# 896 of 2048 columns of the first expert layer as dense products, and one-hot products that pick each slot's value

## The chip, the cores and the metric

The kernel runs on one NeuronCore of one Trainium2 chip. Five engines work side by side, each through its own queue in order: TensorE (PE, matrix products, with its weight loads as PEld), VectorE (DVE), ScalarE (ACT), GpSimd (POOL) and SyncE (SP, which only starts transfers). Transfers run on 16 DMA engines; they come from a queue that SP or ScalarE fills, or from GpSimd's, which alone makes gathers by a list of rows. What is compared is the device time of one execution in microseconds (us), the median of several.

## What is computed

One encoder layer over 256 tokens and 16 meta tokens of width 2048: a gated linear attention and a differential attention, merged and projected by `w_out`, then an expert layer, then a last norm. Only the expert layer, `peer`, is touched. It has 16,384 experts, each a row of `u_tab` and a row of `v_tab`, and 8 heads; a head takes for each token the 16 best experts of a 128 by 128 grid of key pairs:

```python
qb = (xb @ w_q).reshape(TB, PEER_HEADS, 2, PEER_DKEY)
s = jnp.einsum('thpc,hpnc->thpn', qb, sub_keys)
sv, si = lax.top_k(s, K)                       # K = 16
cand = (sv[:, :, 0, :, None] + sv[:, :, 1, None, :]).reshape(TB, PEER_HEADS, K * K)
cidx = (si[:, :, 0, :, None] * PEER_NKEYS + si[:, :, 1, None, :]).reshape(TB, PEER_HEADS, K * K)
cv, ci = lax.top_k(cand, K)
eidx = jnp.take_along_axis(cidx, ci, axis=-1)
g = jax.nn.softmax(cv, axis=-1)
a = jax.nn.gelu(jnp.einsum('thkd,td->thk', u_tab[eidx], xb))
return jnp.einsum('thk,thkd->td', g * a, v_tab[eidx])
```

So each token has 128 slots (8 heads of 16), each slot an expert i * 128 + j. The step that the change rewrites is the inner product of `u_tab[eidx]` with the token's normalized row, 2048 columns for 256 x 128 slots.

## The kernel before

The 256 tokens are two tiles of 128, `tt` = 0 and 1; a tile's tokens lie on the 128 partitions. After the attention branches and the projection by `w_out`, whose result is `hs`, the expert layer runs in these steps.

- **Queries** (`queries`, L778): for each head, products with `w_q` on TensorE (three passes over weights split into high and low parts, L185 and L186), the scores against the sub-keys (L790), and for the first tile `route` at once.
- **Routing** (`route`, L714): top 16 twice over and once more over the 256 sums, nearly all on VectorE, with two casts (L721, L732) and a product (L736) on GpSimd and an exponential (L743) on ScalarE. Its last instruction, L739, writes the 16 row numbers of the head. The second tile's routing needs only the scores `sS1`, which stay in SBUF, and stands between the gathers of the first tile.
- **Gathers** (`gather_dots`, L745): for each slot GpSimd issues one gather (L751) of 128 rows of 2048 floats, 1 MB, and VectorE multiplies them by the normalized tokens `xb` and sums them into one column of `dots` (L754). There are 2 x 128 of them. Six buffers hold rows: three of tag `g` and three of tag `raw`, by turns.
- **Weights** (`weights_of`, L757): gelu of `dots`, times the softmax; then i, j and the weight of each slot are transposed, so that slots lie on the partitions.
- **W0 and W1**: for each token a 128 by 128 matrix with the weight of expert (i, j) at its place, the product of two one-hot matrices over the slots. `build_w0` (L809) makes all its one-hots on ScalarE, and stands between the gathers of the second tile; `build_w1` (L823) shares them between VectorE, GpSimd and ScalarE and comes after the gathers. W0 and W1 take 64 KB of each partition each.
- **The second expert layer** (from L876): for most columns a dense product of W0 and W1 with all of `v_tab`, four accumulators of 368 columns at a time (L924 to L926), the weights split again (L897, L898); for 576 columns gathers of rows (L884) with VectorE's multiply and add (L887). Then the last norm.

The order of instructions of one engine is fixed when the program is built, by a scheduler that follows data and the order in the code. An engine that waits holds up all that stands behind it in its queue. 

Of the kernel before, what the change touches and what calls it, by code (L numbers as in the profile page):

```python
# [20 lines left out]
P = 128  # L21
# [19 lines left out]
def block_kernel(ctx: ExitStack, tc: tile.TileContext, A: dict, out: bass.AP):  # L41
# [12 lines left out]
    s3 = pool("s3")  # L54
    wpc = ExitStack()
    wp = pool("wp", side="right", c=wpc)
# [4 lines left out]
    bt = pool("bt")  # L61
# [28 lines left out]
    mhalf = cc[:, 257:258]  # L90
    vr = c1.tile([58, P], F32, name="vr")
# [545 lines left out]
    wk.close()  # L637


    rp = pool("rp", side="right", c=rgt)  # L640
    ringc = ExitStack()
    ring = pool("ring", bufs=3, side="right", c=ringc)
# [28 lines left out]
    for tt in range(2):  # L671
        nc.gpsimd.dma_start(xb[:, tt, :], A["g_ffn"].to_broadcast([P, D]))
    sk = ring.tile([P, 16, P], F32, tag="g", name="sk")
# [18 lines left out]
    sS1 = rp.tile([P, 8, 2, P], F32, name="sS1")  # L692
# [11 lines left out]
    ngather = [0]  # L704
# [9 lines left out]
    def route(tt, h, s_):  # L714
# [18 lines left out]
        ohx = rp.tile([P, 2, 16, 16], F32, tag="ohx", name="ohx", bufs=1)  # L733
# [12 lines left out]
    def gather_dots(tt, h, ei):  # L746
        for k in range(16):
            i = ngather[0]
            ngather[0] += 1
# [7 lines left out]
    def weights_of(tt):  # L757
# [5 lines left out]
        nc.scalar.activation(dots[tt], dots[tt], AF.Gelu)  # L763
        nc.vector.tensor_mul(gw[tt], gw[tt], dots[tt])  # L764
        ps = pa([P, 3, P])
        nc.tensor.transpose(ps[:, 0, :], ij[tt][:, 0, :], ident)
        nc.tensor.transpose(ps[:, 1, :], ij[tt][:, 1, :], ident)
        nc.tensor.transpose(ps[:, 2, :], gw[tt], ident)  # L768
        r = bt.tile([P, 3, P], F32, tag=f"b{2 + tt}", name=f"slotT{tt}")
        nc.scalar.activation(r, ps, AF.Copy)  # L770
        return r
# [3 lines left out]
    wait = [(None, ring), (None, ring), (None, [4, 5, 6, 7]), (None, [8, 9, 10, 11]), (None, [12, 13, 14, 15])] + [None] * 3  # L775
    eis = {}

    def queries(h):  # L778
# [6 lines left out]
        s0 = rp.tile([P, 2, P], F32, tag="sS0", name="sS0", bufs=2)  # L785
        with tc.high_priority():
            for tt in range(2):
# [4 lines left out]
                nc.scalar.activation(s0 if tt == 0 else sS1[:, h], ps, AF.Copy, scale=rst[tt])  # L792
# [16 lines left out]
    def build_w0(wt, sT, t4):  # L809
        ps = pa([P, 4, P])  # L810
        oh = wp.tile([P, 2, 4, P], F32, tag="hi", name="oh0", bufs=3)
        for q in range(4):
            t = t4 * 4 + q
            for a in range(2):
                nc.scalar.activation(oh[:, a, q], iota, AF.Abs, bias=sT[:, a, t:t + 1], scale=-1.0)
        nc.scalar.activation(oh, oh, AF.Relu, bias=onec, scale=-1.0)
        for q in range(4):
            t = t4 * 4 + q
            nc.scalar.activation(oh[:, 0, q], oh[:, 0, q], AF.Copy, scale=sT[:, 2, t:t + 1])  # L819
            nc.tensor.matmul(ps[:, q, :], lhsT=oh[:, 1, q], rhs=oh[:, 0, q], start=True, stop=True)  # L820
        nc.scalar.activation(wt[:, :, t4 * 4:t4 * 4 + 4], ps.rearrange("p t i -> p i t"), AF.Copy)

    def build_w1(vp, wt, sT, nj, t4):  # L823
        ps = pa([P, 4, P])
        for q2 in range(2):
# [14 lines left out]
            for q in range(2):  # L840
                oi = vp.tile([P, P], F32, tag="oi1", name="oi1", bufs=4)
# [5 lines left out]
    for h in range(8):  # L847
        gather_dots(0, h, eis[0, h])
        eis[1, h] = route(1, h, sS1[:, h])
    w0p = pool("w0p")  # L850
    W0 = w0p.tile([P, P, P], F32, name="W0")
# [142 lines left out]
def host_vectors(inputs):  # L994
# [5 lines left out]
    for nm in ("w_branch_gla", "w_branch_diff", "w_out", "peer_w_q"):  # L1000
        r["c_" + nm] = host_blocks(np.asarray(inputs[nm])[0], 256)
    return r


def host_constants():
# [4 lines left out]
    cf[:, 257] = -0.5  # L1010
    msk = np.zeros((P, 3, T), np.int32)
# [41 lines left out]
```

## Time and profile before

| | us |
|---|---|
| median of 3 runs | 2612.32 (2608.33 to 2615.7) |
| the profiled execution | 2616.36 |
| its span, first to last instruction | 2614.6 |
| TensorE busy | 1889.1 |
| VectorE busy | 2132.0 |
| GpSimd busy | 1266.1 |
| ScalarE busy | 1106.8 |

The page divides the span into 40 slices of 65 us. A row of the views of time has the start in us from the span's start, the duration, the engine, the line and the operation, the tile written and those read, the shape, and how many equal instructions were joined; in brackets stands the idle time of that engine just before, and what ended it. A joined row's duration reaches from the first start to the last end. A matrix product of f32 operands counts as two records. The view of stretches gives the busy time of each engine, the clock that was granted to TensorE as a share of full speed (1.00 is 2.4 GHz, 0.50 is 1.2 GHz), the busy share of the DMA engines, and what they moved.

### The profile page before, as it was taken

What the parts mean: (1) busy time and instruction counts of PE and PEld (TensorE: products, weight loads), DVE (VectorE), ACT (ScalarE), POOL (GpSimd) and SP (SyncE); (2) the same over time, 40 slices, a digit from 0 to 9 for tenths busy, and PEclk for the clock granted to TensorE, in tenths of its full rate; (3) what the DMA queues carried; (4) which work ended last, traced back from release to release, by engine and by line L of the source; (5) the groups of instructions that cost most, each with busy time, mean ns of one, the idle gap of its engine ahead of it and who ended that gap; (6) DMA issues with size and microseconds to landing.
All of it is one profiled execution on the core that took longest, in us unless ns stands there. A gap on an engine that the chain in (4) does not pass through costs nothing. (4 is left out here: it accounts for less than half of the span.)

```text
span 2614.6 us, 37107 instructions
## 1 busy us (share of the span) xinstructions
PE 1889.1 (72%) x13809; PEld 1835.5 (70%) x13809; DVE 2132.0 (82%) x2921; ACT 1106.8 (42%) x2076; POOL 1266.1 (48%) x989
## 2 busy tenths in 40 slices
PE   8999999999999999997500000143006999999997
PEld 7999999999999999997500000132005888999897
DVE  4778877557777775559999999996978899999998
ACT  4565554345655544443200000698006344444444
POOL 1333310000110001028876888885856777777775
PEclk9999999999999999998855555566558999999999
DMA  4445445554444465656699899997993788889886
GB/s 160 146 147 178 146 148 199 187 181 164 165 157 166 167 237 180 227 198 213 227 350 347 322 375 422 421 421 298 418 357 117 263 304 301 315 302 306 302 300 240
DMA packets 110913, 658.38 MB, mean 252 GB/s; under 512 B 14514, under 2 KB 17132, under 8 KB 53116
## 3 DMA queue, kind: packets, MB, share of 16 engines
q0 software_dynamic: 59216, 348.40, 35.2%
q1 hardware_dynamic: 51312, 307.45, 33.8%
q8 instruction: 108, 1.77, 0.3%
q14 instruction: 73, 0.60, 0.1%
q10 hardware_dynamic: 204, 0.17, 0.0%
HBM read 652.78 MB, written 2.10 MB: 250 GB/s over the span
## 5 line engine op out<-in xcount | busy, mean ns | idle before, releaser
L186 DVE TENSOR_TENSOR lo<-raw,hi 128x1024 fp32r<-128x1024 f32 x354 | 453.2, 1281 | 242.7 <-ACT hi L185 240.9
L202 PE MATMUL pm<-hT,lo 128*128 128x256 f32 (+1 forms) x2048 | 577.9, 285 | 7.9 <-DVE lo L186 7.9
L200 PE MATMUL pm<-hT,hi 128*128 128x256 f32 (+1 forms) x2048 | 581.8, 285 | 0.0
L201 PE MATMUL pm<-hT,hi 128*128 128x256 f32 (+1 forms) x2048 | 581.6, 285 | 0.0
L185 ACT ACTIVATE hi<-raw 128x1024 fp32r<-128x1024 f32 x374 | 395.9, 1059 | 363.3 <-PE pm L201 292.5
L202 PEld LDWEIGHTS pm<-hT,lo 128*128 128x128 f32 x2048 | 384.9, 189 | 10.7 <-DVE lo L186 9.0
L200 PEld LDWEIGHTS pm<-hT,hi 128*128 128x128 f32 x2048 | 386.0, 188 | 0.3
L201 PEld LDWEIGHTS pm<-hT,hi 128*128 128x128 f32 x2048 | 386.1, 189 | 0.2
L884 POOL DMA_INDIRECT gv<-in_peer_v_dram,ent x256 | 309.6, 1209 | 140.9 <-DVE hs L887 87.1
L754 DVE SCALAR_TENSOR_TENSOR g<-g,xb 128x2048 f32<-128x2048 f32 x128 | 326.4, 2553 | 15.6 <-DMA g<-in_peer_u_dram,ent 15.3
L768 PE MATMUL pa<-cc,gwt 128*128 128x128 f32 x2 | 0.9, 474 | 462.3 <-DVE gwt L764 462.3
L926 PE MATMUL acc<-vhi,wb 128*128 128x368 f32 x1024 | 334.2, 331 | 0.8 <-DVE wb L898 0.8
L768 PEld LDWEIGHTS pa<-cc,gwt 128*128 128x128 f32 x2 | 0.4, 181 | 462.9 <-DVE gwt L764 462.9
L754 DVE SCALAR_TENSOR_TENSOR gr<-gr,xb 128x2048 f32<-128x2048 f32 x128 | 295.3, 2309 | 28.8 <-DMA gr<-in_peer_u_dram,ent 28.8
L887 DVE SCALAR_TENSOR_TENSOR hs<-gv,gwt,hs 128x576 f32<-128x576 f32 x256 | 280.3, 1095 | 39.3 <-DMA gv<-in_peer_v_dram,ent 35.0
L751 POOL DMA_INDIRECT gr<-in_peer_u_dram,ent x128 | 259.0, 2023 | 78.6 <-DVE gr L754 33.5
L751 POOL DMA_INDIRECT g<-in_peer_u_dram,ent x128 | 250.3, 1956 | 82.4 <-DVE g L754 31.2
L926 PEld LDWEIGHTS acc<-vhi,wb 128*128 128x128 f32 x1024 | 192.4, 189 | 1.0 <-DVE wb L898 1.0
L925 PE MATMUL acc<-vlo,wb 128*128 128x368 f32 x512 | 172.9, 342 | 18.0 <-DVE vlo L917 9.2
L925 PE MATMUL acc<-vlo,wwv 128*128 128x368 f32 x512 | 172.3, 341 | 15.0 <-DVE vlo L917 10.4
L539 POOL DMA_DIRECT2D sw<-dqT x8 | 4.5, 563 | 287.1 <-ACT dqT L552 175.0
L820 PE MATMUL pa<-oh 128*128 128x128 f32 x256 | 58.1, 408 | 104.2 <-ACT oh L819 102.8
(876 smaller groups left out, 4610.6 us busy)
## 6 DMA issues: line engine op xcount, KB each, us to landing
raw<-in_c_w_in_dram SPq DMA_DIRECT2D x128, 1024.0 KB
raw<-in_c_w_branch_gla_dram SPq DMA_DIRECT2D x16, 1024.0 KB
raw<-in_c_w_branch_diff_dram SPq DMA_DIRECT2D x16, 1024.0 KB
raw<-in_c_w_out_dram SPq DMA_DIRECT2D x16, 1024.0 KB
raw<-in_c_peer_w_q_dram SPq DMA_DIRECT2D x11, 1024.0 KB
gv<-in_peer_v_dram,ent POOLq DMA_INDIRECT x256
raws<-in_c_peer_w_q_dram SPq DMA_DIRECT2D x12, 256.0 KB
xt<-in_x_dram SPq DMA_DIRECT2D x2, 1024.0 KB
```

Source lines behind the costliest of these rows:

```text
L185: nc.scalar.activation(hi[:, ks], raw, AF.Copy)
L186: (lo_eng or nc.vector).tensor_sub(lo[:, ks], raw, hi[:, ks].bitcast(F32))
L200: nc.tensor.matmul(ps[b], lhsT=wh, rhs=ah, start=(k == 0), stop=False)
L201: nc.tensor.matmul(ps[b], lhsT=wh, rhs=al, start=False, stop=False)
L202: nc.tensor.matmul(ps[b], lhsT=wl, rhs=ah, start=False, stop=(k == KT - 1))
L751: nc.gpsimd.indirect_dma_start(out=g, out_offset=None, in_=u_tab, in_offset=bass.IndirectOffsetOnAxis(ap=ei[:, k:k + 1], axis=0))
L754: nc.vector.scalar_tensor_tensor(g, g, 1.0, xb[:, tt, :], op0=ALU.mult, op1=ALU.mult, accum_out=dots[tt][:, s:s + 1])
L820: nc.tensor.matmul(ps[:, q, :], lhsT=oh[:, 1, q], rhs=oh[:, 0, q], start=True, stop=True)
L884: nc.gpsimd.indirect_dma_start(out=g, out_offset=None, in_=v_tab, in_offset=bass.IndirectOffsetOnAxis(ap=eis[tt, s // 16][:, s % 16:s % 16 ...
L887: nc.vector.scalar_tensor_tensor(hs[:, tt, DC:], g, gw[tt][:, s:s + 1], hs[:, tt, DC:], op0=ALU.mult, op1=ALU.add)
L925: nc.tensor.matmul(o, lhsT=wh[:, tt, :], rhs=lo[:, ns], start=False, stop=False)
L926: nc.tensor.matmul(o, lhsT=wl[:, tt, :], rhs=hi[:, ns], start=False, stop=last(tt))
```

## The change

The first 896 columns of the first expert layer are no longer gathered. They are computed for all 16,384 experts and all 256 tokens as a dense product, and the value that belongs to a slot is then taken out of it.

- `gather_dots` fetches columns 896 to 2047 of a row (`element_offset`), 1152 floats, 589,824 bytes a gather, into five buffers of one tag; `xb` keeps only these columns.
- A transposed normalized copy of the first 896 columns, `hn`, is made by small products after the third head's queries. The table's first 896 columns come transposed by the host, `c_uT`, as 128 tiles of 128 x 7 x 128 floats (458,752 bytes), through SP's queue into three buffers. For each tile seven products of 128 x 128 by 256 tokens (L911) run in f32; two tiles make a group with one PSUM tile, and ScalarE copies it into `Y`, which is W0 for the first 128 tokens and W1 for the second.
- `pick` takes four tokens at a time. Four products (L782) spread the slots' j over the partitions, ScalarE turns them into one-hots in two passes (L784, L785), four products (L789) select the row j of `Y` for each slot, and four instructions on VectorE (L790) select column i and sum into `dT`. It is called 32 times for each tile.
- `weights_of` adds `dT` to the gathered part; `dots` and the softmax weights are transposed for it, and the result is transposed back.
- W0 can be built only when its `Y` has been read. Both builds are now the same function, `build_w`, with the one-hots shared between VectorE, GpSimd and ScalarE as in `build_w1`.
- To make room, the scores of the second tile and `hs` go to DRAM and come back (ScalarE's queue), pools are opened and closed elsewhere, and the first heads' `w_q` no longer borrows the gathers' buffers.

```diff
-    xb = s4.tile([P, 2, D], F32, tag="s4", name="xb")
+    xb = rp.tile([P, 2, D - DU], F32, name="xb")
+    hn = rp.tile([P, KU, T], F32, name="hn")
...
-    sS1 = rp.tile([P, 8, 2, P], F32, name="sS1")
+    sS1d = [drp.tile([P, 2, P], F32, name=f"sS1d{h}") for h in range(8)]
+    hsd = drp.tile([P, 2, D], F32, name="hsd")
...
-            g = ring.tile([P, D], F32, tag="g", name="g") if i % 2 else wp.tile([P, D], F32, tag="raw", name="gr", bufs=3)
+            g = ring.tile([P, D - DU], F32, tag="g", name="g", bufs=NG)
             nc.gpsimd.indirect_dma_start(out=g, out_offset=None, in_=u_tab,
-                                         in_offset=bass.IndirectOffsetOnAxis(ap=ei[:, k:k + 1], axis=0))
+                                         in_offset=bass.IndirectOffsetOnAxis(ap=ei[:, k:k + 1], axis=0),
+                                         element_offset=DU)
...
+    def pick(tt, sT, t4):
+        pj = pa([P, 4, P])
+        for q in range(4):
+            t = t4 * 4 + q
+            nc.tensor.matmul(pj[:, q, :], lhsT=identr[:, t:t + 1].to_broadcast([P, P]), rhs=jr[:, tt], start=True, stop=True)
+        oj = rp.tile([P, 4, P], F32, tag="ohx", name="ojT", bufs=2)
+        nc.scalar.activation(oj, pj, AF.Abs, bias=mrow, scale=1.0)
+        nc.scalar.activation(oj, oj, AF.Relu, bias=onec, scale=-1.0)
+        pz = pm([P, 4, P])
+        for q in range(4):
+            t = t4 * 4 + q
+            nc.tensor.matmul(pz[:, q, :], lhsT=oj[:, q, :], rhs=Y[tt][:, :, t], start=True, stop=True)
+            nc.vector.scalar_tensor_tensor(pz[:, q, :], iota, sT[:, 0, t:t + 1], pz[:, q, :], op0=ALU.is_equal, op1=ALU.mult,
+                                           accum_out=dT[:, tt, t:t + 1])
...
+    def weights_of(tt, sT):
...
+        nc.vector.tensor_add(dT[:, tt], dT[:, tt], ps[:, 0, :])
+        nc.scalar.activation(dT[:, tt], dT[:, tt], AF.Gelu)
+        nc.vector.tensor_mul(sT[:, 2], dT[:, tt], ps[:, 1, :])
...
+            nc.scalar.dma_start(sS1d[h], s_)
...
     for h in range(8):
         gather_dots(0, h, eis[0, h])
-        eis[1, h] = route(1, h, sS1[:, h])
...
-    sT0 = weights_of(0)
+        s_ = rp.tile([P, 2, P], F32, tag="sS", name="sS", bufs=3)
+        nc.scalar.dma_start(s_, sS1d[h])
+        eis[1, h] = route(1, h, s_)
+
+    for g in range(P // 2):
+        ps = pm([P, 2, T])
+        for b in range(2):
+            ur = ep.tile([P, KU, P], F32, tag="ur", name="ur", bufs=3)
+            nc.sync.dma_start(ur, A["c_uT"][2 * g + b])
+            for k in range(KU):
+                nc.tensor.matmul(ps[:, b, :], lhsT=ur[:, k, :], rhs=hn[:, k, :], start=(k == 0), stop=(k == KU - 1))
+        for tt in range(2):
+            nc.scalar.activation(Y[tt][:, 2 * g:2 * g + 2, :], ps[:, :, tt * P:(tt + 1) * P], AF.Copy)
     for h in range(8):
         gather_dots(1, h, eis[1, h])
-        for t4 in range(4 * h, 4 * h + 4):
-            build_w0(W0, sT0, t4)
-    sT1 = weights_of(1)
...
+    sTs = [slots_of(tt) for tt in range(2)]
+    for tt in range(2):
+        sT = sTs[tt]
+        for t4 in range(32):
+            pick(tt, sT, t4)
+        weights_of(tt, sT)
...
+        if tt == 0:
+            for t4 in range(32):
+                build_w(ep.tile([P, 4, P], F32, tag="ur", name="oi4", bufs=3), W0, sT, nj, t4)
...
-            build_w1(vp, W1, sT1, nj1, t4)
+            build_w(vp.tile([P, 4, P], F32, tag="gv", name="oi4", bufs=NGV), W1, sT1, nj1, t4)
```

How the instructions then stand on an engine is seen from lists of the two programs. On VectorE, before, at the last gathers of the second tile: L754 is the multiply-and-sum, L764 the product with the softmax, L842 and L837 the one-hots of W1's build.

```order
L754 SCALAR_TENSOR_TENSOR gr,gwt<-gr,xb 128x2048 x2
L754 SCALAR_TENSOR_TENSOR g,gwt<-g,xb 128x2048 x2
L754 SCALAR_TENSOR_TENSOR gr,gwt<-gr,xb 128x2048 x16
L764 TENSOR_TENSOR gwt<-gwt 128x128
L864 TENSOR_SCALAR ent<-slotT_16846 128x128
L842 TENSOR_SCALAR oi_16868<-cc,slotT_16846 128x128
L842 TENSOR_SCALAR oi_16871<-cc,slotT_16846 128x128
L842 TENSOR_SCALAR oi_16878<-cc,slotT_16846 128x128
L842 TENSOR_SCALAR oi_16881<-cc,slotT_16846 128x128
L837 TENSOR_TENSOR oj_16886<-cc,slotT_16846 128x256
```

After it, VectorE's queue at the same place: L764 is now the multiply-and-sum, L750 the last instruction of the routing, L790 the selection in `pick`, L802 and L804 are in `weights_of`, L894 is the one-hot in the build of W0.

```order
L764 SCALAR_TENSOR_TENSOR g,gwt<-g,xb 128x1152
L750 SCALAR_TENSOR_TENSOR ent<-ijt 128x16
L923 TENSOR_SCALAR ent<-slotT_17632 128x128
L764 SCALAR_TENSOR_TENSOR g,gwt<-g,xb 128x1152 x170
L790 SCALAR_TENSOR_TENSOR pm,dT<-cc,slotT_17626,pm 128x128 x128
L802 TENSOR_TENSOR dT<-dT,pa 128x128
L804 TENSOR_TENSOR slotT_17626<-dT,pa 128x128
L894 TENSOR_SCALAR oi_18195<-cc,slotT_17626 128x128 x4
L894 TENSOR_SCALAR oi_18213<-cc,slotT_17626 128x128 x4
```

What moved: behind the last gather stood the build of W1; now 128 selections and the build of W0 stand there, and after these a second 128 selections and the build of W1. Ahead of L750 (before: L739) stand 86 multiply-and-sums, and before it was 93.

On TensorE in the changed kernel, from the last product of the dense layer (L911, into PSUM tiles `pm`) on; L789 selects row j of `Y` (here W0) with the one-hot tile `ojT`, and L782 spreads the j of four tokens:

```order
L911 MATMUL pm_17221<-hn_12574,ur_17222 128x256 x7
L911 MATMUL pm_17221<-hn_12574,ur_17231 128x256 x7
L789 MATMUL pm_17646<-W0_15184,ojT_17643 128x128
L789 MATMUL pm_17663<-W0_15184,ojT_17660 128x128
L789 MATMUL pm_17646<-W0_15184,ojT_17643 128x128
L789 MATMUL pm_17663<-W0_15184,ojT_17660 128x128
L789 MATMUL pm_17646<-W0_15184,ojT_17643 128x128
L789 MATMUL pm_17663<-W0_15184,ojT_17660 128x128
L789 MATMUL pm_17646<-W0_15184,ojT_17643 128x128
L789 MATMUL pm_17663<-W0_15184,ojT_17660 128x128
L782 MATMUL pa_17740<-jr_15169,identr_15167 128x128 x4
L782 MATMUL pa_17757<-jr_15169,identr_15167 128x128 x4
```

The products of two calls of `pick` stand by turns, two one-hot tiles a pair, and the spreading for a later pair behind them. On ScalarE the same pairs stand so, behind the last copies of the dense layer (L913; L784 and L785 are the two passes over a one-hot tile):

```order
L913 ACTIVATE W0_15184<-pm_17221 128x256
L913 ACTIVATE W1_15185<-pm_17221 128x256
L784 ACTIVATE ojT_17677<-pa_17672,cc_94 128x512
L784 ACTIVATE ojT_17694<-pa_17689,cc_94 128x512
L785 ACTIVATE ojT_17677<-ojT_17677,cc_94 128x512
L785 ACTIVATE ojT_17694<-ojT_17694,cc_94 128x512
L784 ACTIVATE ojT_17711<-pa_17706,cc_94 128x512
L784 ACTIVATE ojT_17728<-pa_17723,cc_94 128x512
L785 ACTIVATE ojT_17711<-ojT_17711,cc_94 128x512
L785 ACTIVATE ojT_17728<-ojT_17728,cc_94 128x512
```

Nothing stood at either place before; at this point of the program TensorE and ScalarE had the last of W0's one-hots and products.

## Rows read from the trace of the kernel before

**Rows 1.** The page: TensorE's busy tenths in 40 slices of the span.
```profile
PE   8999999999999999997500000143006999999997
```

**Rows 2.** Busy time by stretch; columns as the first line says.
```profile
core 0: us, PE busy (x) PEld busy (x) DVE busy (x) ACT busy (x) POOL busy (x), PEclk, DMA share, GB/s
1200.00:1538.00 338.00, 65.59 (x448) 61.93 (x446) 333.12 (x617) 29.27 (x66) 272.65 (x157) 0.61 0.82 302
1538.00:1801.00 263.00, 48.97 (x217) 43.76 (x217) 243.25 (x215) 142.45 (x400) 228.70 (x107) 0.56 1.01 420
1801.00:1823.00 22.00, 9.80 (x42) 9.02 (x42) 0.63 (x2) 19.92 (x52) 1.39 (x2) 0.63 0.42 175
...
1975.00:2024.00 49.00, 41.88 (x262) 37.05 (x263) 47.00 (x150) 42.63 (x98) 32.42 (x50) 0.94 0.25 81
```

**Rows 3.** Timeline, all engines: the wait for L898 (start, duration, instruction, idle before).
```profile
1822.37 0.42 DVE L898 TENSOR_TENSOR wb<-W,wb 128x256 fp32r<-128x256 f32 x1 [21.72 <-ACT wb L897]
...
1825.28 2.75 POOL L751 DMA_INDIRECT g<-in_peer_u_dram,ent  x1 [22.58 <-DVE g L754]
```

**Rows 4.** Timeline: the end of the last gather's sum, then the first one-hot behind it.
```profile
1975.06 0.09 DVE L754 DVE_READ_ACCUMULATOR gr<-gr,xb 128x1 f32 x1
...
1977.04 1.26 DVE L842 TENSOR_SCALAR oi<-cc,slotT 128x128 f32<-128x128 f32 x4
```

**Rows 5.** Timeline of VectorE: gathered rows multiplied and summed.
```profile
1540.22 0.08 DVE L754 DVE_READ_ACCUMULATOR gr<-gr,xb 128x1 f32 x1
1540.22 2.29 DVE L754 SCALAR_TENSOR_TENSOR g<-g,xb 128x2048 f32<-128x2048 f32 x1
...
1542.43 2.29 DVE L754 SCALAR_TENSOR_TENSOR g<-g,xb 128x2048 f32<-128x2048 f32 x1
```

**Rows 6.** Groups by line, GpSimd, 1200 to 1538: count | busy, mean ns | idle before.
```profile
L751 POOL DMA_INDIRECT g<-in_peer_u_dram,ent x53 | 93.4, 1763 | 33.3 <-DVE g L754 7.0 <-issue 4.9 <-DVE sv L711 4.7
```

**Rows 7.** Timeline of TensorE: 128x128 f32 products at full clock.
```profile
1168.57 0.61 PE L790 MATMUL pa<-skT,pqt 128*128 128x128 f32 x4
1169.01 0.71 PE L685 MATMUL pa<-cc,sk 128*128 128x128 f32 x5
```

**Rows 8.** DMA view of 1560 to 1600, then of 2100 to 2300 (packets, MB, share).
```profile
DMA packets 2312, 16.84 MB, mean 421 GB/s; under 512 B 256, under 2 KB 256, under 8 KB 256
...
DMA packets 13696, 61.27 MB, mean 306 GB/s; under 512 B 2142, under 2 KB 2142, under 8 KB 13552
...
q1 hardware_dynamic: 6681, 35.24, 51.2%
q0 software_dynamic: 6999, 25.82, 37.1%
```

**Rows 9.** Timeline of GpSimd's gather issues; last L884's durations (min/median/max).
```profile
1541.41 1.91 POOL L751 DMA_INDIRECT gr<-in_peer_u_dram,ent  x1 [0.30 <-issue]
...
1770.95 0.94 POOL L751 DMA_INDIRECT gr<-in_peer_u_dram,ent  x1 [0.30 <-issue]
...
L884 POOL DMA_INDIRECT gv<-in_peer_v_dram,ent x256: 945/1146/2227, 2021.2 to 2587.3; - x128
```

**Rows 10.** Timeline of ScalarE: evaluations of 512 columns from PSUM, of 128 and 1024 from SBUF.
```profile
1811.43 0.65 ACT L821 ACTIVATE W<-pa 128x512 f32<-128x512 f32 x1
1811.91 2.22 ACT L815 ACTIVATE oh<-cc,slotT 128x128 f32<-128x128 f32 x7
1813.95 0.66 ACT L821 ACTIVATE W<-pa 128x512 f32<-128x512 f32 x1
...
1814.72 2.25 ACT L816 ACTIVATE oh<-oh,cc 128x1024 f32<-128x1024 f32 x2
1816.80 0.76 ACT L819 ACTIVATE oh<-oh,slotT 128x128 f32<-128x128 f32 x2
```

**Rows 11.** Timeline of VectorE: two instructions of 256 elements from PSUM.
```profile
1082.73 0.88 DVE L668 SCALAR_TENSOR_TENSOR hg<-pa,vec,hg 128x256 fp32r<-128x256 f32 x2 [1.26 <-ACT hg L667]
```

**Rows 12.** Timeline of TensorE in the build of W1.
```profile
1996.00 1.81 PE L844 MATMUL pa<-oi,oj 128*128 128x128 f32 x12 [0.19 <-DVE oi L842]
```

More of the change, by code (lines that the diff above doesn't have):

```diff
@@ L53, in block_kernel @@
     cst = pool("cst")
-    s3 = pool("s3")
+    bt = pool("bt")
+    s3c = ExitStack()
+    s3 = pool("s3", c=s3c)
     wpc = ExitStack()
-    wp = pool("wp", side="right", c=wpc)
+    wp = wr = pool("wp", side="right", c=wpc)
+    drp = pool("drp", space=bass.MemoryType.DRAM)
     psA = ctx
@@ L637, in block_kernel @@
     wk.close()
+    rgt.close()
+    wpc.close()
+    KU = 7
+    DU = KU * P
+    rgt = ExitStack()
     rp = pool("rp", side="right", c=rgt)
-    ringc = ExitStack()
-    ring = pool("ring", bufs=3, side="right", c=ringc)
+    ring = pool("ring", side="right", c=rgt)
+    wpc = ExitStack()
+    wp = pool("wp2", side="right", c=wpc)
+    wr = pool("wr2", side="right", c=wpc)
     hs = s3.tile([P, 2, D], F32, tag="s3", name="hs")
     ssq = cst.tile([P, 2, 8], F32, name="ssq")
-    xb = s4.tile([P, 2, D], F32, tag="s4", name="xb")
+    xb = rp.tile([P, 2, D - DU], F32, name="xb")
+    hn = rp.tile([P, KU, T], F32, name="hn")
     hg = [None] * KT
@@ L703, in block_kernel @@
     u_tab = A["peer_u"][0]
-    ngather = [0]
+    NG = 5
     def top16(vo, io, src, n):
@@ L755, in gather_dots, with slots_of @@
                                            accum_out=dots[tt][:, s:s + 1])
-    def weights_of(tt):
+    def slots_of(tt):
+        r = bt.tile([P, 3, P], F32, tag=f"b{2 + tt}", name=f"slotT{tt}")
+        ps = pa([P, 2, P])
+        for a in range(2):
+            nc.tensor.transpose(ps[:, a, :], ij[tt][:, a, :], ident)
+        nc.scalar.activation(r[:, 0:2], ps, AF.Copy)
+        nc.scalar.activation(jr[:, tt], ij[tt][:, 1, :], AF.Copy)
+        return r
+    def pick(tt, sT, t4):
[13 more added lines that the diff above has]
+    def weights_of(tt, sT):
         rc = rp.tile([P, 8], F32, tag="rcs", name="rcs", bufs=2)
@@ L799, in block_kernel, with build_w @@
     for tt in range(2):
-        nc.vector.scalar_tensor_tensor(xb[:, tt, :], hs[:, tt, :], rst[tt], xb[:, tt, :], op0=ALU.mult, op1=ALU.mult)
+        nc.vector.scalar_tensor_tensor(xb[:, tt, :], hs[:, tt, DU:], rst[tt], xb[:, tt, :], op0=ALU.mult, op1=ALU.mult)
+    nc.scalar.dma_start(hsd, hs)
     for h in range(1, 8):
         queries(h)
+        if h == 2:
+            dg = []
+            for tt in range(2):
+                d_ = wp.tile([P, P], F32, tag="hi", name="dgr", bufs=3)
+                nc.vector.tensor_scalar(d_, ident, rst[tt], None, op0=ALU.mult)
+                dg.append(d_)
+            for k in range(KU):
+                ps = pa([P, T])
+                for tt in range(2):
+                    nc.tensor.matmul(ps[:, tt * P:(tt + 1) * P], lhsT=hs[:, tt, k * P:(k + 1) * P], rhs=dg[tt], start=True,
+                                     stop=True)
+                nc.scalar.activation(hn[:, k, :], ps, AF.Copy, scale=vec[:, gf + k:gf + k + 1])
+    identr = rp.tile([P, P], F32R, name="identr")
+    nc.scalar.activation(identr, ident, AF.Copy)
+    jr = rp.tile([P, 2, P], F32R, name="jr")
+    dT = rp.tile([P, 2, P], F32, name="dT")
+    nj0 = rp.tile([P, P], F32, name="nj0")
+    wpc.close()
     ph0.close()
     ph1.close()
-    W1E = "pav"
[L809 to L823, printed above, removed]
+    s3c.close()
+    wp01 = pool("w01")
+    epc = ExitStack()
+    ep = pool("ep", side="right", c=epc)
+    W0 = wp01.tile([P, P, P], F32, name="W0")
+    W1 = wp01.tile([P, P, P], F32, name="W1")
+    Y = [W0, W1]
+    W1E = "pav"
+    def build_w(oi4, wt, sT, nj, t4):
         ps = pa([P, 4, P])
```

60 lines of the change are left out of this document (30 added, 30 removed).

## The prediction

> **What bounds the kernel now.** I read TensorE's slices first [rows 1], then the busy time of each engine by stretch [rows 2], then single instructions inside the stretches. The first 1200 us (18 slices) and the last 590 us keep TensorE nine tenths busy, and the change hardly touches them. Between 1200 and 1975 us lies what it does touch: TensorE is almost idle, and VectorE, GpSimd and the DMA queues carry the 256 gathers of expert rows. The table [rows 2] splits that stretch. From 1200 to 1538 VectorE is full (333.12 of 338 us): it finds the top-k entries and multiplies and sums gathered rows as they come; GpSimd is fairly full too (272.65 us). From 1538 to 1801 no routing is left and the DMA engines are full at 420 GB/s. From 1801 to 1823 everything waits for one VectorE instruction, L898, that stands in its queue ahead of the remaining gathers and needs the whole of W0 [rows 3]; VectorE waits 21.72 us there, and GpSimd, whose ring is full, 22.58 us. Then the gathers end at 1975.1 [rows 4], and W1 is built in the open, at VectorE's pace (47.00 of 49 us busy). Everything behind the last gather, W1's build included, takes 2614.6 - 1975.1 = 639.5 us.
>
> So the sum goes in three moves: when the routing ends, when the last gather ends, and what then stands between the last gather and that unchanged tail.
>
> **Routing, 1200 to 1538.** The gathered row shrinks from 2048 to 1152 columns. A multiply-and-sum of 2048 starts every 2.21 us [rows 5]; taking off the 0.08 us of the accumulator read, the rest goes with the columns: 2.13 x 1152/2048 + 0.08 = 1.28 us (an estimate from those rows). By the program's order VectorE has 93 of these ahead of the last routing instruction before, and 86 now. If VectorE stays the bound, it saves 93 x 2.21 - 86 x 1.28 = 95 us, and the routing ends at 1443. GpSimd can't follow that: its 272.65 us shrink only by about eight gather issues of 1.8 us [rows 6], to 258 us, and its casts and multiplies sit between VectorE's steps, so both are in the chain by turns. The lower end is 1443, 1458 is GpSimd without one gap; with a little waiting for each other I take 1470, and 1490 as the upper end. The scores of the second half of the tokens now go to DRAM and back on ScalarE's queue; ScalarE was busy 29.27 of these 338 us, which hides it. 13 of the 64 dense groups lie here as well, on a TensorE busy for 65.59 us; they cost nothing.
>
> **From the routing's end to the last gather.** What is left is 170 multiply-and-sums, some 165 gathers of 128 x 4608 B = 97.3 MB to be moved, and of the dense layer 51 groups, with 102 tiles of 458,752 B, the first three loaded ahead: 45.4 MB. Three engines share this.
> - VectorE: 170 x 1.28 = 218 us.
> - TensorE: two f32 products of 128x128 by 128 columns, two records each, take 1169.01 - 1168.57 = 0.44 us at full clock [rows 7]; one is 0.22 us, and would be 0.44 at half clock. A dense product streams 256 columns, 0.44 us; 14 a group, 6.1 us; 51 groups, 310 us.
> - DMA: 97.3 + 45.4 = 142.7 MB. One queue of 8 KB rows reached 421 GB/s [rows 8]: 339 us. The later stage with a gather queue and an SP queue together moved 306 GB/s at a share of 51.2% + 37.1%, or 347 GB/s if full: 411 us. Ours is full like the first and mixed like the second; it is nearer to the first, since in the second the engines idled 12% and a packet's time then includes waiting. I take 400 GB/s, 357 us, and keep both ends.
> - GpSimd: an issue takes 1.91 us and then 0.30 idle, in step with the multiply's 2.21 us, but 0.94 us where it began just ahead of VectorE's instruction, and 1.15 us in the middle of the later gathers of 576 columns [rows 9]. I read the 1.91 as waiting for VectorE's instruction to end; with instructions of 1.28 us an issue fits in each. The other reading, 2.2 us whatever the width, gives 170 x 2.2 = 374 us, inside the DMA's bounds.
>
> So DMA bounds: 1470 + 357 = 1827 for the last gather (range 1443 + 339 = 1782 to 1490 + 411 = 1901). The 22 us wait of L898 is gone, since W0 is now built later. What is late next is TensorE, done some 47 us earlier. The gain is 1975 - 1827 = 148 us.
>
> The Trainium skill ("SBUF — State Buffer", Who interferes with whom) says that VectorE and GpSimd share one pair of SBUF ports under an exclusive lock, while DMA has ports of its own. It agrees with the lockstep of [rows 9], and by it the GpSimd term would never bind here.
>
> **What now follows the last gather.** VectorE's order puts everything else behind the 170: 128 picks of the first tokens, the build of W0, 128 picks of the second, then W1's build. Before, only W1's build stood there.
> - Picks run as 64 calls of four tokens, in pairs. A pair's two one-hot tiles are the only two buffers, so ScalarE writes the next pair only after TensorE has read this one. A turn is: two evaluations from PSUM of 128x512 at 0.48 us, two more from SBUF at 0.61 us, which lies on the line between 0.29 us for 128 and 1.04 us for 1024 columns [rows 10], 2.18 us together; then eight products of 0.22, 1.76 us; then the fall-through of the last of each, 0.16 us of ScalarE (0.65 - 0.48 of its duration) and 0.39 of TensorE (0.61 - 0.22). Sum 4.5 us, or 2.25 a call. VectorE's part hides beside it: two of 256 elements from PSUM take 0.88 us [rows 11], 0.4 each, so about 0.35 for 128 with the accumulator read, 2.8 us a pair. PSUM's four buffers let four calls run ahead of the last gather. Left: 28 + 32 = 60 calls, 135 us.
> - W0's build, now like W1's: six products (twelve records) every 1.81 + 0.19 = 2.00 us, one a token [rows 12], 128 tokens in 43 us. Its one-hot work before lay beneath the gathers.
> - Entry and exit of the two pick loops, one more round of transposes, gelu and product: from the last gather to the first build took 1977.04 - 1975.06 = 2 us [rows 4], and there are now about five such hand-overs, 10 us. The 13 weight conversions moved behind another step in the w_out stage add 2 us at most.
>
> Sum 135 + 43 + 12 = 190 us. Against 148 gained that is 42 us lost. New span 1827 + 190 + 639.5 = 2656.5. The profiled execution ran 2616.4 us with a span of 2614.6, and lies 4 us above the median of 2612.3; so the median would be 2656.5 + 1.8 - 4 = **2654 us**.
>
> **The rivals.**
> - *The picks run at the engines' own rate* (faster). If ScalarE, TensorE and VectorE overlap across pairs after all, the slowest, VectorE, sets 1.4 us a call: 60 x 0.85 = 51 us less, 2603. The place is the one-hot ring; the change wins from 1.55 us a call down (148 - 55 = 93 us for 60 calls). For it: ScalarE's next evaluation needs only the older of the two tiles. Against: the order of products alternates between the pair's tiles, so that both come free at the end of the eight. With the early ends for routing and DMA as well, 2558.
> - *A pick's product takes twice as long*. TensorE would be busy only 1.76 of 4.5 us; in the 22 us stretch in which it was busy for 9.80 us its mean clock was 0.63 of full [rows 2], and at half clock a product is 0.44 us. 30 pairs x 1.76 = 53 us more, 2707. The moving operand Y[:, :, t] moreover takes one float out of every 512 bytes; no row here shows that. The Trainium skill ("SBUF — State Buffer", note on cachelines in Door 1) says that such reads, each on a new 16-byte line, pay a penalty, without giving it; it speaks against this change, and if it doubled the product it would give the same 2707.
> - *The two queues together reach only 347 GB/s*: 54 us more, 2708.
>
> **How the numbers follow.** Forecast 0.50 (2615 to 2690), fast picks 0.20, slow products 0.16, slow queues 0.14. To leave out no more than 2 in 10 the range goes from 2585, past the fast picks with a little of the early ends, to 2715. A measurement of this kernel tells about 0.3% from no change, 8 us: faster is below 2604.5, which takes half of the fast picks and a little of the forecast's low side with the early ends, 0.19; same, to 2620, takes most of the rest of these, 0.12; slower 0.69.
>
> **What would show it.** The last gather's multiply ends near 1827 with DMA full before it; multiply-and-sums of 1.28 us; dense groups of 14 products every 6 us; ScalarE's evaluations in pairs every 4.5 us, VectorE idle for a third of that; a 43 us build of W0 between the picks; 640 us behind the last pick. It is wrong if picks come under 1.55 us a call, if the last gather ends before 1785, or if the dense products run at half clock (12.2 us a group, 622 us: then TensorE ends after the gathers).

## The result, and the profile after

The change makes the kernel slower: 2720.52 us median (2714.64 to 2725.61, 4 runs) against 2612.65 us; the ratio is 1.0413, with a 95% interval of 1.0388 to 1.0439. The forecast was 2654 us with a range up to 2715, so the sign was right and the size was not.

The page's slices of the kernel after, for TensorE, VectorE, TensorE's granted clock and the DMA engines:

```profile
PE   8999999999999999987695999989898899999996
...
DVE  4878887567777765579897666664745999899998
...
PEclk9999999999999999998797999985755999999998
DMA  4444445554445654677799999960001488889997
```

Against [rows 1], TensorE is now busy nearly throughout. But in slices 28, 30 and 31 (of 67.8 us each, so 1831 to 1899 and 1967 to 2102 us) the clock is near half, VectorE is at four to five tenths, and the DMA engines rest. The view of stretches, cut where the steps of the new program begin, says what they are; it answers to [rows 2]:

```profile
core 0: us, PE busy (x) PEld busy (x) DVE busy (x) ACT busy (x) POOL busy (x), PEclk, DMA share, GB/s
1200.00:1452.00 252.00, 165.99 (x887) 146.93 (x888) 236.85 (x603) 40.98 (x100) 193.11 (x149) 0.84 0.81 281
1452.00:1812.80 360.80, 329.84 (x1455) 270.88 (x1454) 232.38 (x345) 36.28 (x107) 201.12 (x166) 0.99 1.01 400
1812.80:1924.00 111.20, 99.91 (x357) 80.90 (x357) 51.91 (x252) 38.53 (x61) 0.00 (x0) 0.51 0.00 1
1924.00:1975.00 51.00, 42.36 (x291) 36.89 (x291) 45.33 (x161) 42.02 (x102) 29.59 (x44) 0.94 0.01 2
1975.00:2087.00 112.00, 100.26 (x356) 80.88 (x356) 52.09 (x253) 37.56 (x60) 0.00 (x0) 0.50 0.00 1
2087.00:2140.00 53.00, 44.72 (x297) 40.93 (x297) 49.63 (x159) 44.06 (x104) 33.67 (x50) 0.90 0.35 126
2140.00:2712.00 572.00, 534.74 (x3034) 509.17 (x3033) 536.11 (x649) 256.41 (x401) 426.77 (x385) 0.98 0.88 302
```

In order: the routing beside gathers; gathers and dense groups together; the picks of the first 128 tokens; the build of W0; the picks of the second; the build of W1; the second expert layer. From 1452 to 1812.8 the DMA engines are full at 400 GB/s, the rate that the forecast took. The two stretches of picks take 111 and 112 us, and no engine is full there: VectorE 52 us, ScalarE 38 us. TensorE's 100 us are modelled ends of products that follow one another at a distance; its weight loads, one ahead of each product, are busy for 81 us. Its clock is 0.51 and 0.50, the lower of its two levels, which it left for the upper in the build of W0 (0.94) and in the stretches on either side.

### The profile page after: what moved, and what is told of

It reads as the page before. It is cut to its first block, busy times and chain, and to the rows that moved or that the text cites. A ratio compares the mean times of both kernels' runs of the same rounds, so it can differ in the third digit from the quotient of the medians.

```text
span 2712.9 us, 43399 instructions
## 1 busy us (share of the span) xinstructions
PE 2490.5 (92%) x16401; PEld 2328.8 (86%) x16401; DVE 2039.6 (75%) x3589; ACT 1107.1 (41%) x1991; POOL 1081.7 (40%) x1031
## 4 chain that ended last, share of the span: by engine, by line
PE 52%; DVE 14%; issue 12%; POOL 10%; DMA 9%; ACT 2%; POOLq 0%; DVEq 0%; ACTq 0%; SPq 0%
PE pm L203 12%; PE pm L201 12%; PE pm L202 12%; DMA gv<-in_peer_v_dram,ent 7%; POOL g L760 6%; PE pm L789 4%; DVE g L764 3%; DVE hs L956 2%; PE pa L782 2%; DVE oi L894 2%; PE acc L994 1%; DVE pm L790 1%; PE acc L995 1%; POOL gv L953 1%; PE pm L217 1%
## 5 line engine op out<-in xcount | busy, mean ns | idle before, releaser
L764 DVE SCALAR_TENSOR_TENSOR g<-g,xb 128x1152 f32<-128x1152 f32 x256 | 374.6, 1466 | 140.0 <-DMA g<-in_peer_u_dram,ent 139.6
L911 PE MATMUL pm<-hn,ur 128*128 128x256 f32 x1792 | 410.5, 387 | 36.9 <-DMA ur<-in_c_uT_dram 30.4
L911 PEld LDWEIGHTS pm<-hn,ur 128*128 128x128 f32 x1792 | 338.3, 193 | 108.0 <-DMA ur<-in_c_uT_dram 26.4
L760 POOL DMA_INDIRECT g<-in_peer_u_dram,ent x256 | 310.0, 1211 | 213.3 <-DVE g L764 152.7
L956 DVE SCALAR_TENSOR_TENSOR hs<-gv,gwt,hs 128x576 f32<-128x576 f32 x256 | 288.8, 1128 | 26.5 <-DMA gv<-in_peer_v_dram,ent 23.5
L790 DVE SCALAR_TENSOR_TENSOR pm<-cc,slotT,pm 128x128 f32<-128x128 f32 x256 | 90.8, 355 | 120.8 <-PE pm L789 119.2
L913 ACT ACTIVATE W<-pm 128x256 f32<-128x256 f32 x128 | 41.6, 380 | 324.4 <-PE pm L911 320.9
L789 PE MATMUL pm<-W,ojT 128*128 128x128 f32 x512 | 156.8, 448 | 14.2 <-ACT ojT L785 3.7
L789 PEld LDWEIGHTS pm<-W,ojT 128*128 128x128 f32 x512 | 120.3, 309 | 45.9 <-DVE pm L790 38.1
```

The costliest lines, as they stand in the source:

```text
L789: nc.tensor.matmul(pz[:, q, :], lhsT=oj[:, q, :], rhs=Y[tt][:, :, t], start=True, stop=True)
L911: nc.tensor.matmul(ps[:, b, :], lhsT=ur[:, k, :], rhs=hn[:, k, :], start=(k == 0), stop=(k == KU - 1))
L956: nc.vector.scalar_tensor_tensor(hs[:, tt, DC:], g, gw[tt][:, s:s + 1], hs[:, tt, DC:], op0=ALU.mult, op1=ALU.add)
```

## What one turn of the picks consists of

The timeline of the kernel after, all engines, over one pair of calls of `pick` (start and duration in us, the idle time before and its end in brackets):

```profile
1823.81 1.26 ACT L784 ACTIVATE ojT<-pa,cc 128x512 f32<-128x512 f32 x2 [4.76 <-PE pm L789]
...
1824.55 1.97 PE L782 MATMUL pa<-jr,identr 128*128 128x128 f32 x8 [0.41 <-ACT ojT L784]
1824.96 1.33 ACT L785 ACTIVATE ojT<-ojT,cc 128x512 f32<-128x512 f32 x2
...
1826.21 0.97 PEld L789 LDWEIGHTS pm<-W,ojT 128*128 128x128 f32 x4
1826.31 5.07 PE L789 MATMUL pm<-W,ojT 128*128 128x128 f32 x16
1827.09 0.35 DVE L790 SCALAR_TENSOR_TENSOR pm<-cc,slotT,pm 128x128 f32<-128x128 f32 x1 [2.50 <-PE pm L789]
...
1827.51 0.36 DVE L790 SCALAR_TENSOR_TENSOR pm<-cc,slotT,pm 128x128 f32<-128x128 f32 x1
1827.56 0.93 PEld L789 LDWEIGHTS pm<-W,ojT 128*128 128x128 f32 x4 [0.38 <-DVE pm L790]
...
1828.39 0.35 DVE L790 SCALAR_TENSOR_TENSOR pm<-cc,slotT,pm 128x128 f32<-128x128 f32 x1 [0.46 <-PE pm L789]
...
1828.86 0.93 PEld L789 LDWEIGHTS pm<-W,ojT 128*128 128x128 f32 x4 [0.37 <-DVE pm L790]
...
1831.05 0.69 ACT L784 ACTIVATE ojT<-pa,cc 128x512 f32<-128x512 f32 x1 [4.76 <-PE pm L789]
```

A pair takes 1831.05 - 1823.81 = 7.24 us, 3.62 us a call. ScalarE writes its two one-hot tiles in 2.5 us (1823.81 to 1826.29), near the 2.18 + 0.16 = 2.34 us of the forecast. Then come the eight products, and they don't follow one another: a weight load for the next two waits for VectorE (`<-DVE pm L790`), VectorE's selection waits for the product (`<-PE pm L789`), and so by turns. A turn of two products takes 1828.86 - 1827.56 = 1.30 us; four of them 5.2 us, where the forecast had 1.76 us for eight products on end. The view of line L789 gives it for the whole run (durations in ns as min/median/max; then the idle time by what ended it, in us and times):

```profile
L789 PE MATMUL pm<-W,ojT x512: 393/405/583, 1809.5 to 2086.0; 128*128 128x128 f32 x171
...
its engine sat idle before it (us, times) until:
  DVE pm L790: 41.6, 101
```

What makes the products wait is the code's order, as e1 below shows. In `pick` each product writes one quarter of the PSUM tile `pz`, and VectorE's selection for that quarter reads and overwrites it before the next product is written down. The trace shows weight loads and products waiting on VectorE 101 times, although the next product needs another quarter of the tile; whether a tile for each token would also have freed them, no run here tests. The list of instructions ahead of the prediction shows the products of two calls by turns, but not these waits.

The same wait kept the picks from running ahead of the last gather, where the forecast had four calls done by then:

```profile
1809.55 1.12 PE L789 MATMUL pm<-W,ojT 128*128 128x128 f32 x4 [0.47 <-ACT W L913]
...
1813.18 0.72 PEld L789 LDWEIGHTS pm<-W,ojT 128*128 128x128 f32 x4 [2.92 <-DVE pm L790]
```

One product of each of two calls is done; the next waits for a selection, and the selections stand behind the last gather's sum, which ends at 1812.7.

## The experiments

Three explanations were at hand for 3.62 us a call instead of 2.25: A, the turns between TensorE and VectorE; B, TensorE's half clock; C, the read of `Y[:, :, t]`, one float in every 512 bytes.

**e1: the products ahead of the selections.** The loop over four tokens is cut in two.

```diff
             nc.tensor.matmul(pz[:, q, :], lhsT=oj[:, q, :], rhs=Y[tt][:, :, t], start=True, stop=True)
+        for q in range(4):
+            t = t4 * 4 + q
             nc.vector.scalar_tensor_tensor(pz[:, q, :], iota, sT[:, 0, t:t + 1], pz[:, q, :], op0=ALU.is_equal, op1=ALU.mult,
```

> Only pick changes: the four products of a call stand ahead of its four selections on VectorE, instead of taking turns with them. Theory A (each product waits for VectorE's selection on the same PSUM tile, 1.30 us a turn of two products): the turns fall away, and a call goes from 3.62 us to 1.75 us, VectorE's four selections, if TensorE's clock comes back, or 2.7 us if it stays at 0.50; 62 calls, so 2604 to 2663 us. Theory B (the half clock alone sets the loop): a call stays over 3.2 us, 2695 us or more. Theory C (the strided read of Y makes a product slow): the products keep their time, 0.65 us each, and a call stays near 3.3 us, 2700 us.

Measured: 2628.28 us, ratio to before 1.0056 (1.0039 to 1.0072): 92 us of the 108 lost come back from this reordering. The timeline of e1, one call:

```profile
1841.36 0.65 PEld L782 LDWEIGHTS pa<-jr,identr 128*128 128x128 f32 x4
...
1841.80 0.69 ACT L784 ACTIVATE ojT<-pa,cc 128x512 f32<-128x512 f32 x1 [0.74 <-PE pm L789]
1841.80 0.36 DVE L792 SCALAR_TENSOR_TENSOR pm<-cc,slotT,pm 128x128 f32<-128x128 f32 x1 [0.78 <-PE pm L789]
...
1841.99 1.94 PE L789 MATMUL pm<-W,ojT 128*128 128x128 f32 x8
...
1843.58 0.75 PE L782 MATMUL pa<-jr,identr 128*128 128x128 f32 x4
...
1843.97 0.69 ACT L784 ACTIVATE ojT<-pa,cc 128x512 f32<-128x512 f32 x1 [0.73 <-PE pm L789]
```

Four products now follow one another without a wait, from 1841.99 to the spreading product at 1843.58, 0.40 us each, and a call takes 1843.97 - 1841.80 = 2.17 us. The stretches of picks in e1 (columns as above):

```profile
1817.00:1883.00 66.00, 64.73 (x350) 61.26 (x348) 43.62 (x255) 42.73 (x60) 0.00 (x0) 1.00 0.00 1
1930.00:2000.00 70.00, 68.81 (x370) 64.97 (x370) 43.87 (x253) 44.18 (x64) 0.00 (x0) 1.00 0.00 1
```

The clock is 1.00 with no other change, so it came back with the turns gone. A stands; how much of the 92 us is the clock, e1 alone doesn't tell, and e7 is for that. The expected 1.75 us a call was not reached: TensorE is full (64.73 of 66 us), with products of 0.40 us where [rows 7] had 0.22.

**e2: five one-hot tiles instead of two**, on top of e1.

```diff
-        oj = rp.tile([P, 4, P], F32, tag="ohx", name="ojT", bufs=2)
+        oj = ring.tile([P, D - DU], F32, tag="g", name="ojT", bufs=NG)[:, :4 * P].rearrange("p (q s) -> p q s", q=4)
```

> As e1, and the one-hot tiles lie in the five gather buffers instead of two of their own. Theory of the prediction (the two one-hot tiles bind ScalarE and TensorE into one chain): e1 alone stays at about 2.25 us a call or more, and here it falls to VectorE's 1.75, so some 30 us below e1. Theory A (the turns were all): the same as e1 within 8 us.

Measured: 2642.50 us, ratio 1.0107 (1.0090 to 1.0124), 14 us slower than e1. The first picks stood ready when the gathers ended in e1; here their tiles are those of the last gathers, and the first product starts at 1822.6 in place of 1814.0. Nothing was gained elsewhere: the picks' products begin over 183.6 us (1822.6 to 2006.2), and over 184.6 us in e1. So the two one-hot tiles, which the forecast made the loop's bound, did not bind it once the turns were gone and a product took 0.40 us.

**e3: the same picks with neighbouring floats.** The turns are left in; a product reads `Y[tt][:, t, :]` in place of `Y[tt][:, :, t]`. The values that it picks are not those of the slots; what the kernel leaves out is the right selection, and only its time is read.

> As the changed kernel, but a product in pick reads Y[:, t, :], 128 neighbouring floats, in place of Y[:, :, t], one float out of every 512 bytes; it picks from the wrong values, so that part of the result is left out. Theory A and B: nothing changes, a pair of calls 7.25 us, span 2713 us. Theory C (the stride doubles a product): a pair loses eight times 0.2 us or more, to 5.6 us, and the span falls by 50 us to 2663.

Measured: 2716.73 us, one run. ScalarE's first one-hot of a pair in e3:

```profile
1833.23 1.26 ACT L784 ACTIVATE ojT<-pa,cc 128x512 f32<-128x512 f32 x2 [4.76 <-PE pm L789]
...
1840.47 1.26 ACT L784 ACTIVATE ojT<-pa,cc 128x512 f32<-128x512 f32 x2 [4.76 <-PE pm L789]
```

A pair takes 7.24 us as before. With the turns there and the clock at 0.53 from 1813 to 1920, the stride costs nothing that shows. C is no cause of the loss of this kernel.

**e7: the clock, held up.** One product more for each token, `ident` by `iota`, written into the used tile `pj`, read by nobody.

> As the changed kernel, with one more product per token in pick whose result nobody reads; they stand behind the eight products of a pair, while ScalarE makes the next one-hots. Theory A (turns between TensorE and VectorE): the clock comes back to 1.00 and the turn of 1.30 us shrinks only by the product's half-clock share, 0.2 us, so a pair goes from 7.25 to about 6.4 us, span 2687. Theory B (the half clock sets the loop): a pair falls to 4.5 us, 2630. If the clock stays at 0.50 the fillers cost at most 8 x 0.44 us a pair less ScalarE's 2.2 us: up to 8.5 us, 2750.

Measured: 2742.07 us, one run. The stretch of the first picks, then ScalarE's first one-hots of two pairs, and between them the fillers (L790 in this run) and three weight loads:

```profile
1812.00:1920.00 108.00, 97.64 (x524) 78.15 (x522) 46.90 (x217) 32.29 (x52) 0.00 (x0) 0.91 0.01 2
```

```profile
1851.25 1.27 ACT L784 ACTIVATE ojT<-pa,cc 128x512 f32<-128x512 f32 x2 [4.95 <-PE pm L789]
...
1851.99 2.05 PE L790 MATMUL pa<-cc 128*128 128x128 f32 x16 [0.40 <-ACT ojT L784]
...
1854.21 0.72 PEld L789 LDWEIGHTS pm<-W,ojT 128*128 128x128 f32 x4
...
1856.71 0.73 PEld L789 LDWEIGHTS pm<-W,ojT 128*128 128x128 f32 x4 [0.47 <-DVE pm L791]
...
1857.90 0.73 PEld L789 LDWEIGHTS pm<-W,ojT 128*128 128x128 f32 x4 [0.46 <-DVE pm L791]
...
1858.68 1.27 ACT L784 ACTIVATE ojT<-pa,cc 128x512 f32<-128x512 f32 x2 [4.95 <-PE pm L789]
```

The clock was 0.91 here, against 0.51, and a pair took 1858.68 - 1851.25 = 7.43 us all the same; a turn shrank from 1.30 to 1857.90 - 1856.71 = 1.19 us. So the half clock is worth 0.11 us a turn, 0.4 us a pair, some 14 us over 32 pairs. The fillers used that up, so the 6.4 us that A expected was missed too: the first weight load came 1854.21 - 1851.25 = 2.96 us behind ScalarE's start, against 1826.21 - 1823.81 = 2.40 us without them. What the clock costs in this part of a pair, where the fillers stand, e7 doesn't tell. A pair of 4.5 us, as B expected, is far off: in the turns the clock is a small part, and the waits are the rest.

**e5: neighbouring floats without the turns.** On top of e1, ScalarE stores the dense products with the token as the outer index.

```diff
-            nc.scalar.activation(Y[tt][:, 2 * g:2 * g + 2, :], ps[:, :, tt * P:(tt + 1) * P], AF.Copy)
+            nc.scalar.activation(Y[tt][:, :, 2 * g:2 * g + 2], ps[:, :, tt * P:(tt + 1) * P].rearrange("p b t -> p t b"), AF.Copy)
...
-            nc.tensor.matmul(pz[:, q, :], lhsT=oj[:, q, :], rhs=Y[tt][:, :, t], start=True, stop=True)
+            nc.tensor.matmul(pz[:, q, :], lhsT=oj[:, q, :], rhs=Y[tt][:, t, :], start=True, stop=True)
```

> As e1 (products ahead of the selections), and ScalarE stores the dense products with the token as the outer index, so that a product in pick reads 128 neighbouring floats; the values are the same. In e1 a product took 0.40 us at full clock against 0.22 us for one with neighbouring operands. Theory A plus stride: the product falls to 0.22 us, a call from 2.18 us to VectorE's 1.75 us, 60 calls, some 26 us below e1: 2602 us. Rival (the 0.40 us is PSUM or the weights, not the stride): within 8 us of e1. If ScalarE's stores of two floats in every 512 bytes are slow they show in its 0.33 us a copy.

Measured: 2585.17 us, ratio 0.9892 (0.9866 to 0.9918): faster than both kernels, and 1.1% faster than before. TensorE in e5:

```profile
1924.74 1.10 PE L789 MATMUL pm<-W,ojT 128*128 128x128 f32 x8
1925.60 0.64 PE L782 MATMUL pa<-jr,identr 128*128 128x128 f32 x4
1926.08 1.12 PE L789 MATMUL pm<-W,ojT 128*128 128x128 f32 x8
```

Four products now take 1925.60 - 1924.74 = 0.86 us, 0.215 each, and a call 1.34 us. So the stride does cost, nearly a doubling from 0.22 to 0.40 us, once nothing else holds the product: e1 showed the 0.40, e5 takes it away, and in e3 it lay hidden behind the turns at half clock. The two stretches of picks in e5:

```profile
1817.00:1859.00 42.00, 38.51 (x318) 37.57 (x318) 40.77 (x253) 36.75 (x55) 0.00 (x0) 0.96 0.01 1
1903.00:1952.00 49.00, 46.20 (x394) 44.65 (x394) 43.22 (x259) 44.17 (x70) 1.91 (x4) 1.00 0.01 1
```

They last 42 and 49 us, and VectorE and TensorE are both nearly full, so little more is to be had from their order. The 43 us gained on e1 lie here: these stretches are 136 - 91 = 45 us shorter.

**e6, e10, e11: hiding the first picks among the last gathers.** All on top of e5: the first tile's one-hot tiles take turns with gathered rows in their ring, so that picks stand among the last gathers. e6 has five buffers for rows and three for dense tiles; e10 three and five; e11 four and four.

> As e5, and the first tile's picks stand among the last 48 gathers of the second tile (their one-hot tiles take turns with the gathered rows in the ring), and the transposes of the slots stand behind the dense groups, so that TensorE need not wait for the routing's end. Hidden are up to 32 calls, 50 us, if the dense layer is done some 100 us before the last gather: 2550 us. If the dense layer and the gathers end together, as in the changed kernel, the gathers wait for the picks and nothing is gained: 2600 us or more.

> As e6, but three buffers for gathered rows and five for dense tiles, and the first tile's picks among the last 32 gathers: the dense layer should get more of the DMA engines and end earlier, so that the picks hide. If it ends by 1740: some 40 us below e5, 2545. If three buffers starve the gathers instead, their end moves back and it is above e6's 2625.

> As e10 with four buffers for gathered rows and four for dense tiles. e10 ended the dense layer at 1697 and the gathers only at 1962, with a DMA share near 0.7; e6, with five and three, ended the dense layer at 1798 and held the gathers back to 1895. If there is a point between at which both hold, the gathers end before 1850 with the first tile's picks hidden: 2560 us. If fewer rows in flight simply cost DMA throughput, the result lies between e6's 2625 and e10's 2710.

Measured: e6 2625.53 us (1.0050, 1.0035 to 1.0065), e10 2710.14 us (1.0362, 1.0335 to 1.0389), e11 2635.24 us (1.0072, 1.0047 to 1.0097). The views of single lines say why (durations, then first and last start). The first tile's products in e6:

```profile
L795 PE MATMUL pm<-W,ojG x256: 275/421/553, 1797.9 to 1896.5; 128*128 128x128 f32 x128
```

and the dense products, then the multiply-and-sums, of e10:

```profile
L919 PE MATMUL pm<-hn,ur x1792: 379/379/767, 1307.4 to 1697.1; 128*128 128x256 f32 x200
```

```profile
L765 DVE SCALAR_TENSOR_TENSOR g<-g,xb x256: 1334/1359/9920, 1188.8 to 1962.0; 128x1152 f32<-128x1152 f32 x128
```

In e6 the picks could not begin before 1797.9, when the dense layer was done, and the gathers behind them waited: the last sum started at 1893.1 instead of 1815. In e10 the dense layer was done by 1697 (64 groups in 390 us, the 6.1 us each that [rows 7] give at full clock), but with three buffers the gathers dragged on to 1962, with the DMA engines at a share of 0.75 from 1700 to 1800. In e11 the dense layer was done at 1713 and the last sum started at 1892.5; its time lies between. In none of the three divisions did both end early: where the dense layer did, it was at the gathers' cost.

**e8 and e9: the slots' transposes behind the dense groups, and eight blocks of columns in place of seven.** In e8 the transposes take their PSUM tile from the dense groups' pool, so that TensorE need not wait for them at the routing's end; e9 adds `KU = 8`. Both stand on e5.

> As e5, and the slots' transposes take a PSUM tile of the dense groups' pool, so that they stand behind the dense groups on TensorE, which then need not wait for the routing's end at 1452. If the DMA engines have room before 1452 (share 0.81 there), the last gather ends up to 25 us earlier: 2560 us. If they are what bounds the dense tiles too, within 8 us of e5's 2585.

> As e8 with 1024 dense columns in place of 896: gathers of 1024 columns (16.8 MB less), dense tiles of 524,288 bytes (8.4 MB more), dense products 64 groups of 16, 443 us of TensorE instead of 387. If DMA is the bound up to the last gather, 8.4 MB at 400 GB/s, so 21 us below e8. If TensorE becomes the bound (1320 + 443 = 1763 at the earliest, before the gathers' end), nothing or a loss.

Measured: e8 2584.61 us (0.9883, 0.9855 to 0.9910), e9 2588.30 us (0.9891, 0.9857 to 0.9925). The stretch from the routing's end to 1815, e8 first, then e9:

```profile
1452.00:1815.00 363.00, 323.28 (x1439) 266.66 (x1437) 233.84 (x346) 36.84 (x109) 205.27 (x172) 1.00 1.01 400
```

```profile
1452.00:1815.00 363.00, 353.01 (x1600) 299.67 (x1599) 206.03 (x334) 33.68 (x100) 181.89 (x165) 1.00 0.98 385
```

e8's time can't be told from e5's, but e8 does not test what it was made for, since TensorE was still held before the routing's end. Its wait in e5, then in e8:

```profile
1452.98 0.69 PE L772 MATMUL pa<-cc,ijt 128*128 128x128 f32 x2 [28.04 <-DVE ijt L748]
```

```profile
1446.83 1.12 PE L782 MATMUL pa<-jr,identr 128*128 128x128 f32 x4 [18.86 <-ACT ojT L784]
```

In place of the transposes, a spreading product of the first picks now stands ahead of the dense groups and waits for ScalarE. From 1452 on the DMA engines are full in both, at a share of 1.01; what a TensorE that is free before 1452 would gain stays open. In e9 the last multiply-and-sum starts 22 us earlier than in e8 (1792.6 against 1814.9), as reckoned, but TensorE, busy for 353 of 363 us, starts its last dense product only at 1819.6, and the picks need it. At seven blocks the two end near each other (1808 and 1815 in e8); with an eighth TensorE ends last, after a wait of 14 us like e8's.

## Why the prediction was wrong

Its own steps, against the kernel after:

| step | forecast | measured |
|---|---|---|
| routing ends | 1470 (1443 to 1490) | 1452 |
| last gather's sum | 1827 (1782 to 1901) | 1812.7 |
| rate of the DMA engines there | 400 GB/s | 400 GB/s |
| picks behind the last gather | 60 calls, 135 us | 64 calls, 112.5 + 113.2 = 226 us |
| W0's build and the hand-overs | 55 us | 48 us |
| everything behind the second picks | 639.5 us | 626 us |
| span | 2656.5 | 2712.9 |

- **Right**: the stages, and that the gain at the gathers (162 us by the trace, 148 forecast) is less than what comes out from beneath them. A multiply-and-sum of 1152 columns took this in the kernel after:

```profile
L764 DVE SCALAR_TENSOR_TENSOR g<-g,xb x256: 1305/1358/4607, 1188.4 to 1811.4; 128x1152 f32<-128x1152 f32 x128
```

that is 1.36 us long, and the last ones, at the end of the gathers, began every 1.38 to 1.39 us, where the forecast had 1.28. This lies off the path, since DMA set the pace. A gather issue on GpSimd fell to 1.21 us in the mean, from 1.96 and 2.02 for the two tags before, which agrees with the forecast's reading of [rows 9] that it waits for VectorE's instruction to end. That the two engines lock each other out is more than those rows show: the issue of 1541.41 ended at 1543.32, 0.9 us into VectorE's next instruction [rows 5], which kept its pace of 2.21 us. Nor would such a lock have left the GpSimd term harmless: 170 issues of 0.94 us and 170 instructions of 1.28 us one behind the other are 377 us, more than the 357 us of the DMA. Right too is the chain of a pair, one-hots and products one behind the other: ScalarE waits 4.76 us each time for the last product.
- **Wrong at no cost here**: TensorE was to be done with the dense layer 47 us ahead of the last gather. Its last dense product starts at 1808.7, 4 us before the gathers' end, since it waited 26.9 us for the slots' transposes at the routing's end and, over the whole layer, 57 us for tiles that come through the same full DMA engines. So the last gathers left no room for the picks, which e6 ran into.
- **The term that was mis-sized**: the step on the picks, 4.5 us a pair. Its eight products were costed at 8 x 0.22 us on end; they run in four turns with VectorE, 1.30 us each. VectorE's selections were written off as lying beside the products. The step named their duration but not who waits for them. For the same reason no call was finished ahead of the last gather, where the step had four. Together this is 226 - 135 = 91 us, more than the whole miss of 56 us in the span; the other steps, forecast too long by 14, 7 and 13 us, took part of it back. The median missed by 66 us: the profiled execution lay 4 us above the median before, and lies 6 us below it now.
- **The rival that came near by its number**: a pick's product twice as long, 2707 us. That was luck, since its two reasons don't carry it. The clock did fall to 0.50, as it reckoned, but in the turns e7 shows that to be worth some 0.4 us a pair, where it had 1.76; and the stride, by e3, nothing in this kernel. The Trainium skill's note in "SBUF — State Buffer", Door 1, that each access on a new 16-byte line pays a penalty, agrees with e1 and e5 all the same: 0.40 us against 0.215 for the same product. The length of a line no run here tests. The third rival, 347 GB/s, did not come: the trace has 400.
- **The rival on the faster side** put the point of decision at 1.55 us a call with the other steps as forecast, and 2603 us for 1.4 us a call. e5 has 1.34 us and 2585, and is faster than before; e1 has 2.17 us and 2628, and is slower. On the line between these two the kernel before, 2613, lies near 1.87 us a call (an estimate), so the point came later than 1.55; the other steps were 34 us shorter than forecast. What decided the case is the cost of a call, and the order of the code and the layout of `Y` set it: the order alone (e1) was not enough.
- **Open**: why the tail behind the second picks is 13 us shorter than before. TensorE's idle time ahead of the products with `vlo` in the last layer is smaller after than before, 20 us against 33, but no run isolates it.

## What to carry to other kernels

Where engines pass parts of one PSUM tile to each other inside a loop, cost the loop by who waits for whom, not by each engine's busy time: a selection after each product made a turn of 1.30 us out of two products that take 0.80 us on end in e1, and writing the products first, all else equal, gave 92 us back. The half clock in such a stretch was here a sign of waits more than a cause: it went to 1.00 by itself in e1, and held up to 0.91 in e7 it gave little. And a step that is taken out from under a long transfer has to be paid for in full, so look at the order behind the last transfer before looking at the bytes saved.

## What was not expected of the hardware

A product of 128x128 by 128 columns in f32 that reads one float in every 512 bytes took 0.40 us at full clock, and 0.215 us with neighbouring floats; at half clock the pair of calls took 7.24 us either way. ScalarE's copies that store two floats in every 512 bytes were hardly slower than those in longer pieces: 0.39 us in e5 in the middle against 0.38 us in e1. And the SP queue's tiles and the gathers together reached 400 GB/s with rows of 4608 and 3584 bytes, near the 421 GB/s of 8 KB rows [rows 8], not the 347 that the forecast worked out for a full later stage.
